# Two-layer trunk: quarters at the layers' turn in two-tile pieces, the state product in the inner product's bank, three yT sets

## The chip, the cores and the metric

The kernel runs on one core of one Trainium2 chip. The metric is the device time of one execution in microseconds (us), lower is better. A core has TensorE (matmuls; PE in rows), VectorE (DVE), ScalarE (ACT), GpSimd (POOL) and SyncE (SP), each with its own instruction stream in program order; SyncE here issues most DMAs. Matmul results land in PSUM banks, everything else lies in SBUF, and GpSimd cannot be given work on PSUM here: all its operands are SBUF tiles.

## The reference

1024 tokens of width 1024 pass two layers. Each computes `h = RMSNorm(x)*(1+scale)+shift`, `y = mixer(h)`, `x = x + gate*RMSNorm(y)`. Layer 0 mixes by differential attention, layer 1 by retention, which in chunks of 64 tokens is:

```python
inner = einsum("bnihd,bnjhd->bnhij", q, k) * intra_decay       # gamma^|i-j|
inner_out = einsum("bnhij,bnjhe->bnihe", inner, v)
def step(state, qkv):
    cross = einsum("bihd,bhde->bihe", q_c * query_decay, state)  # gamma^i
    state = chunk_decay * state + einsum("bjhd,bjhe->bhde", k_c * key_decay, v_c)
out = head_rms_norm(inner_out + cross)     # 4 heads, q/k 256 wide, v 512 wide
y = silu(g) * out ; result = y @ w_out
```

All is float32; the kernel keeps the accuracy by splitting each float32 operand in a high and a low float16 part and adding three products (high·high, high·low, low·high).

## The kernel before, in words

Tokens are handled in eight tiles of 128 rows. One program runs layer 0, the turn to layer 1, layer 1's four heads one after the other, and the last output projection. TensorE holds nearly all the time, and the other engines prepare for it.

**The turn.** After attention, `out0(t)` makes the output projection of tile t (48 matmuls of 512 columns on line 562), squares and sums it (ACT, line 574), takes the root on POOL (lines 576, 577, 140), adds the residual (DVE, 579), and normalizes the rows once more into `x1` (ACT 291, POOL 292 and 140, DVE 614). `out0_yT(t)` turns tile t's mixer output first: two casts and one transposing DMA on SP (line 602). `out0_hT(g)` then makes layer 1's input: `x1` of four token tiles is transposed on TensorE (line 310), scaled and shifted on ACT (629) and cast to two float16 parts, plain (`hA`, `hB`) and as sums and differences (`hS`, after subtracts on DVE, lines 630 to 634); the casts are lines 640 (ACT) and 641 (DVE). Layer 1's input projections use a two-by-two block scheme with seven products instead of eight, hence these sums, and hence sums of weight blocks too: four adds on POOL (line 759) for each set of columns, before the casts of the weights (ACT 772, DVE 773). `PRODUCTS` gives the order of the seven: the first two need `hA` and `hB` only, the third and fourth need `hS`.

The order of all this is a string: each letter is a function, each digit its argument, and each engine executes in that order, apart from what the scheduler interleaves:

```python
order = ("... b7 f0 y5 o3 o4 y6 o5 h0 y7 o6 o7 h1")   # y: out0_yT, o: out0, h: out0_hT
```

**Retention.** For each head come the seven products of the q/k columns (line 799, 256 columns each), those of v, and those of the gate. In the gate's seven steps, behind the second half of a step, stands a step of retention, `retention(n)`: `scores` of a span (line 946, times a decay table on DVE, line 952, then casts 953 and 954), `state` of the span before (line 968: keys times decayed values, added to a running state by DVE 974 or 976, cast 978 and 979), and `outputs` (inner product, line 989, in one bank; state product, line 999, in another). ACT brings the state product times the query decay to SBUF (1003), DVE adds the inner product (1004), and DVE normalizes (1007).

**The tail.** `gated` multiplies with silu(gate). The last projection (line 1120) needs `yT(t)`: two transposing DMAs from DRAM `y_d` (heads 0 to 2, line 1106) and two from head 3's own result (1108), in one of two buffers that bear the tags of `qT` and `kT`, so tile 0's may start when head 3 has read `qT` for the last time. Its weights arrive through SP (line 1092) in sixteen pieces, and are cast on ACT (1096) and DVE (1097), in the order in which the first token tile needs them: 36 matmuls for output half 0, 36 for half 1, then twelve each with head 3.

## Time and profile before

| | before |
|---|---|
| median of 3 runs | 1405.28 us (1404.12 to 1405.83) |
| the profiled execution | 1402.77 us, span 1400.8 us |
| TensorE busy | 1299.1 us, granted clock 0.981 |
| VectorE, ScalarE, GpSimd busy | 929.3, 670.0, 261.0 us |

The profiled execution is one run, 2.5 us below the median. The span is the traced part of it. A view of waits lists, for each engine, how long it stood idle and what it waited for last; a timeline lists an engine's instructions in order of time, consecutive ones of a line together, with the idle time ahead in brackets; a table of stretches gives each engine's busy time in it and TensorE's granted clock (1.0 is the upper of its two levels, 2.4 GHz; 1.2 GHz is 0.5).

### The profile page before, as it was taken

The numbers are of one execution on the slowest core, as the hardware profiler recorded it, in microseconds if no ns is written. First come the engines' busy times: TensorE is split into PE (matmuls) and PEld (weight loads), VectorE is DVE, ScalarE is ACT, GpSimd is POOL, SyncE is SP. The second block draws the span as 40 slices with busy tenths as digits, with TensorE's granted clock in tenths as the row PEclk, the third lists the DMA queues.
The fourth block names the chain that finished last, engine by engine and source line by source line (L and its number), as shares of the span: only waits on it lengthen the run. The fifth ranks groups of instructions, "written<-read, shape, count | busy, mean of one in ns | idle before, by whom it ended". The sixth has DMA issues, their size and how long they took to land. (4 is left out here: it accounts for less than half of the span.)

```text
span 1400.8 us, 21197 instructions
## 1 busy us (share of the span) xinstructions
PE 1299.1 (93%) x8273; PEld 776.8 (55%) x8273; DVE 929.3 (66%) x1734; ACT 670.0 (48%) x1250; POOL 261.0 (19%) x318
## 2 busy tenths in 40 slices
PE   4899999899999997896899999999999999799998
PEld 2445455445545444355786658665866586544443
DVE  4866996997986777666558765876587648831011
ACT  4855544654654655366354644454445445720000
POOL 2000110101101222520223122322232220100000
PEclk9999999999999999898999999999999999999999
DMA  9723554656452466631212242223222333474350
GB/s 298 244 69 70 131 120 115 143 126 134 102 128 52 126 148 132 151 109 49 69 60 76 84 128 62 76 83 117 73 76 74 103 92 121 119 154 97 97 121 30
DMA packets 244372, 152.60 MB, mean 109 GB/s; under 512 B 142840, under 2 KB 233136, under 8 KB 244272
## 3 DMA queue, kind: packets, MB, share of 16 engines
q1 hardware_dynamic: 241168, 140.24, 38.8%
q0 software_dynamic: 3104, 11.02, 2.6%
q8 instruction: 64, 1.05, 0.3%
q14 instruction: 36, 0.29, 0.1%
HBM read 101.95 MB, written 14.68 MB: 83 GB/s over the span
## 5 line engine op out<-in xcount | busy, mean ns | idle before, releaser
L773 DVE SCALAR_TENSOR_TENSOR w<-raw,w 128x1024 f16<-128x1024 f32 x82 | 121.8, 1489 | 88.7 <-ACT w L772 88.6
L331 PE MATMUL ps_mm<-w,hT 128*128 128x512 f16 x768 | 175.7, 379 | 0.0
L1120 PE MATMUL ps_mm<-wo,yT 128*128 128x512 f16 x768 | 167.8, 382 | 4.2 <-DMA yT<-y_d 4.2
L799 PEld LDWEIGHTS <-hS 128*128 128x128 f16 x1536 | 150.1, 98 | 20.9
L759 POOL TENSOR_TENSOR raw<-raw,raw 128x1024 f32<-128x1024 f32 x48 | 126.8, 2642 | 186.7 <-DVE w L773 183.5
L319 PE MATMUL ps_mm<-hT,w 128*128 128x512 f16 x624 | 142.2, 379 | 0.0
L799 PE MATMUL ps_mm<-w,hS 128*128 128x256 f16 x1152 | 130.3, 273 | 0.0
L1120 PEld LDWEIGHTS <-yT 128*128 128x128 f16 x768 | 75.3, 98 | 96.6 <-DMA yT<-y_d 5.2
L511 ACT ACTIVATE sb<-sb,mx 128x128 f32<-128x128 f32 (+7 forms) x128 | 98.2, 768 | 63.5 <-DVE mx L504 62.9
L331 PEld LDWEIGHTS <-hT 128*128 128x128 f16 x768 | 74.2, 98 | 82.5
L799 PEld LDWEIGHTS <-w 128*128 128x128 f16 x744 | 75.2, 101 | 78.3 <-issue 13.6
L772 ACT ACTIVATE w<-raw 128x1024 f16<-128x1024 f32 x82 | 85.8, 1049 | 39.8 <-issue 15.0
L575 DVE TENSOR_TENSOR po<-ps_mm,gp 128x512 f32<-128x512 f32 x16 | 11.1, 691 | 132.0 <-ACT junk L574 132.0
L562 PE MATMUL ps_mm<-w_o,yT 128*128 128x512 f16 x384 | 93.4, 394 | 4.8 <-DVE x L575 3.6
L319 PEld LDWEIGHTS <-w 128*128 128x128 f16 x624 | 60.1, 98 | 67.5
L504 DVE CUSTOM_DVE_ANT_0 sb<-ps_sc,table 128x512 f32<-128x512 f32 (+3 forms) x128 | 73.2, 584 | 33.5 <-PE ps_sc L501 26.1
L574 ACT ACTIVATE junk<-ps_mm 128x512 f16<-128x512 f32 x32 | 19.0, 595 | 154.5 <-PE ps_mm L1120 145.0
L799 PE MATMUL ps_mm<-w,hA 128*128 128x256 f16 x768 | 86.6, 273 | 0.0
L799 PEld LDWEIGHTS <-hA 128*128 128x128 f16 x768 | 75.1, 98 | 9.9
L292 POOL TENSOR_SCALAR ss<-ss 128x1 f32<-128x1 f32 x48 | 19.1, 398 | 300.2 <-ACT junk L291 288.5
L799 PE MATMUL ps_mm<-hS,w 128*128 128x512 f16 (+1 forms) x312 | 63.0, 362 | 12.0 <-ACT held L807 12.0
L169 DVE SCALAR_TENSOR_TENSOR acc<-raw,cond,acc 128x256 f32<-128x256 f32 x140 | 65.7, 480 | 7.8 <-DMA raw<-in_ada_w 6.2
(202 smaller groups left out, 2247.0 us busy)
## 6 DMA issues: line engine op xcount, KB each, us to landing
raw<-in_ret_w_in SPq DMA_DIRECT2D x60, 512.0 KB, 3.6
raw<-in_ada_w SPq DMA_DIRECT2D x40, 512.0 KB, 6.6
raw<-in_da_w_in SPq DMA_DIRECT2D x16, 1024.0 KB, 5.8
raw1o<-in_ret_w_out SPq DMA_DIRECT2D x16, 512.0 KB, 4.5
y_d<-y SPq DMA_DIRECT2D x6, 1024.0 KB, 4.7
x<-in_x SPq DMA_DIRECT2D x8, 512.0 KB, 7.5
raw<-in_ada_w SPq DMA_DIRECT2D x4, 1024.0 KB, 5.3
raw_o<-in_da_w_out SPq DMA_DIRECT2D x4, 1024.0 KB, 5.1
```

Source lines behind the costliest of these rows:

```text
L169: nc.vector.scalar_tensor_tensor(out=acc, in0=parts[k], scalar=cond[:, k : k + 1], in1=acc, op0=ALU.mult, op1=ALU.add)
L292: nc.gpsimd.tensor_scalar(out=ss[:, 3:4], in0=ss[:, 0:1], scalar1=scale / n, scalar2=eps, op0=ALU.mult, op1=ALU.add)
L319: nc.tensor.matmul(ps, w[:, k, wi, lo : lo + P], hT[k][g][:, xi, :], start=(k == 0 and wi == 0 and xi == 0), stop=(k == NK - 1 and wi == 1),)
L331: nc.tensor.matmul(ps, hT[k][g][:, xi, j * P : (j + 1) * P], w[:, k, wi, :], start=(k == 0 and wi == 0 and xi == 0), stop=(k == NK - 1 and ...
L504: nc.vector.tensor_tensor_reduce(out=sb[:, c, k], in0=ps[c][:, 0:n], in1=table[:, S - L + lo : S - L + lo + n], scale=-es, scalar=(3.0e38 ...
L511: nc.scalar.activation(out=sb[:, c, 0:L], in_=sb[:, c, 0:L], func=AF.Exp, scale=-1.0, bias=mx[:, m0 + c : m0 + c + 1], accum_out=z[:, 4 * ...
L562: nc.tensor.matmul(ps, yT(yi, k), wo[k // 4][:, k % 4, wi, n * 512 : (n + 1) * 512], start=(k == 0 and yi == 0 and wi == 0), stop=(k == NK ...
L759: add = lambda o, x: nc.gpsimd.tensor_tensor(out=r[o], in0=r[o], in1=r[x], op=ALU.add)
L772: nc.scalar.activation(out=w[:, :, 0, :], in_=r[name], func=AF.Copy, scale=SW)
L773: nc.vector.scalar_tensor_tensor(out=w[:, :, 1, :], in0=r[name], scalar=SW, in1=w[:, :, 0, :], op0=ALU.mult, op1=ALU.subtract)
L799: nc.tensor.matmul(ps[:, pc], l, r, start=(first and i == 0 and k == 0 and wi == 0 and xi == 0), stop=(k == 3 and wi == 1), skip_group_che ...
L1120: nc.tensor.matmul(ps[n], yT1[t][:, yi, k, :], wo1[k // 4, n][:, k % 4, wi, :], start=(k == 0 and yi == 0 and wi == 0), stop=(k == 15 and ...
```

## The change

Three parts are changed at once.

1. **The turn.** `out0_hT` is called four times, for two token tiles each, instead of twice for four. Its pieces take buffers of their own (`early` and `ys` tags that are done with) in place of attention's "v" buffers. The subtracts run on GpSimd for the first three calls and on VectorE for the last. `hS` is laid out in other tiles. The order string has the four calls spread: one behind tile 3's projection, one behind tile 4's, one behind tile 6's, one at the end.
2. **Retention.** The last span (two tiles) becomes two of one. The state product is the first to be written into the inner product's bank, and the inner product adds to it; the passes of lines 1003 and 1004 are gone. For that, the query decay is folded in a second decay table for the scores and in the norm's epsilon. Scores come earlier: those of the first span in v's products, the others between the two halves of a gate step; state and outputs follow the second half. There is a fourth `kN`, and one more state per head.
3. **The tail.** `yT` has three sets in turn (four `held` buffers, and the `qT` and `kT` tags) and takes six transposing DMAs per tile (8, 8, 4 and 4 blocks from `y_d`, 4 and 4 from head 3) in place of four.

The diff, cut to its core:

```diff
-SST = 2.0**4
+SA1 = 2.0
...
-SPANS = ((0, 2), (2, 1), (3, 1), (4, 1), (5, 1), (6, 2))
+SPANS = ((0, 2), (2, 1), (3, 1), (4, 1), (5, 1), (6, 1), (7, 1))
+DECS = RC + P + 3
...
-        out[h, :, RC : RC + 2] = np.exp(log_gamma * i) * (RQK**-0.5 * SA * SV / (SQK1 * SST))
...
+        out[h, :, RC : RC + P] = np.where(p // CHUNK <= u1 // CHUNK, c * SA1 * np.exp(log_gamma * (np.abs(u1 - p) - u1)), 0.0)
+        out[h, :, RC + P] = HEAD_EPS * np.exp(-2.0 * log_gamma * p[:, 0])
...
-    def out0_hT(g):
-        if g == 0:
+    def out0_hT(j):
+
+        if j == 0:
...
-        n = slice(g * 256, (g + 1) * 256)
-        for k in range(4):
-
-            t = att.tile([P, 8, 256], F32, name="hq", tag="v", bufs=2)
+        n = slice(j * P, (j + 1) * P)
+        for kh in range(2):
+
+            pa, ta, ba = (early, "qs", 2) if j == 0 else (ys, f"y{2 * j - 2 + kh}", 1)
+            pb, tb, bb = (early, "ks", 2) if j < 2 else (ys, f"y{2 * j - 4 + kh}", 1)
+            t = pa.tile([P, 4, 2, P], F32, name="hq", tag=ta, bufs=ba)
+            t2 = pb.tile([P, 4, 2, P], F32, name="hq2", tag=tb, bufs=bb)
             for i in range(2):
...
+                for kk in range(2):
+                    k = 2 * kh + kk + 4 * i
+                    for b in range(2):
+                        c = (2 * kk + b) * P
+                        nc.tensor.transpose(out=ps[:, c : c + P], in_=xns[2 * j + b][:, k * P : (k + 1) * P], identity=ident)
+                    m = mods[1, k]
+                    nc.scalar.activation(
...
+            eng = nc.vector if j == 3 else nc.gpsimd
+            for i in range(2):
+                eng.tensor_tensor(out=t2[:, i], in0=t[:, 1], in1=t[:, 3 * i], op=ALU.subtract)
+            eng.tensor_tensor(out=t2[:, 2], in0=t[:, 0], in1=t2[:, 1], op=ALU.subtract)
+            eng.tensor_tensor(out=t2[:, 3], in0=t[:, 2], in1=t2[:, 2], op=ALU.subtract)
...
-        "o1 b5 a6 a7 b6 y4 o2 b7 f0 y5 o3 o4 y6 o5 h0 y7 o6 o7 h1"
+        "o1 b5 a6 a7 b6 y4 o2 b7 f0 y5 o3 h0 o4 y6 h1 o5 y7 o6 h2 o7 h3"
...
-            for c in range(NC - 1):
-                kn = ret.tile([P, 2, 2, 2, P], F16, name="kN", tag="kN", bufs=3)
+            for c in range(NC):
+                kn = ret.tile([P, 2, 2, 2, P], F16, name="kN", tag="kN", bufs=4)
...
+                    if n == 5 and u == 1:
+                        scores(*SPANS[0])
...
                 o = av()
+                if t0 > 0:
+                    c, u = part(t)
+                    for m in range(2):
+                        for qi, si in ((0, 0), (0, 1), (1, 0)):
+                            nc.tensor.matmul(
+                                o, st["qT"][:, c, m, qi, u], sts[t0][:, m, si, :],
+                                start=(m == 0 and qi == 0 and si == 0), stop=False,
+                            )
...
-                    nc.scalar.activation(out=dst, in_=x, func=AF.Copy, scale=st["dec"][:, RC + i : RC + i + 1])
-                    nc.vector.tensor_tensor(out=dst, in0=o, in1=dst, op=ALU.add)
...
+                s0, eps = (SA1 * SV, st["dec"][:, RC + P : RC + P + 1]) if t0 > 0 else (SA * SV, HEAD_EPS)
+                r = row_rsqrt(o, RV, 1.0 / s0**2, eps)
+                nc.vector.tensor_scalar(out=y1[t // 4][:, t % 4, :], in0=o, scalar1=r, scalar2=1.0 / s0, op0=ALU.mult, op1=ALU.mult)
...
+                    if u == 0 and n + 1 < len(SPANS):
+                        scores(*SPANS[n + 1])
                     if u == 1:
-                        retention(n)
+                        if n + 1 < len(SPANS):
+                            state(*SPANS[n])
+                        outputs(*SPANS[n])
...
-        yT = ret.tile([P, 2, 16, P], F16, name="yT", tag=("qT", "kT")[t % 2], bufs=1)
+        if t % 3 == 0:
+            ps_ = [held(F16, [P, 8, P]) for _ in range(4)]
+        else:
+            yt = ret.tile([P, 4, 8, P], F16, name="yT", tag=("qT", "kT")[t % 3 - 1], bufs=1)
+            ps_ = [yt[:, i] for i in range(4)]
+        for i in range(2):
+            for b in range(2):
+                if i == 0:
+                    nc.sync.dma_start(out=ps_[b], in_=y_d[:, t, b, 0:2, :].rearrange("p h e -> p (h e)"), transpose=True)
+                else:
+                    nc.sync.dma_start(out=ps_[2 + b][:, 0:4, :], in_=y_d[:, t, b, 2, :], transpose=True)
...
-            nc.sync.dma_start(out=yT[:, b, 12:16, :], in_=last_y[t][:, b, :], transpose=True)
+            nc.sync.dma_start(out=ps_[2 + b][:, 4:8, :], in_=last_y[t][:, b, :], transpose=True)
```

Where the instructions stand. First POOL's stream at the turn. Before, the four adds of weight blocks (line 759) stand ahead of the root of tile 3's norm (lines 576, 577, 140), while the attention of the last heads ends:

```order
L759 TENSOR_TENSOR raw_6161<-raw_6161,raw_6165 128x1024
L759 TENSOR_TENSOR raw_6165<-raw_6165,raw_6167 128x1024
L759 TENSOR_TENSOR raw_6167<-raw_6167,raw_6161 128x1024
L759 TENSOR_TENSOR raw_6163<-raw_6163,raw_6167 128x1024
L597 DMA xres<-in_x 128x2x1024
L549 TENSOR_TENSOR sso<-sso,z 128x2
L576 TENSOR_TENSOR ss<-ss 128x1
L550 TENSOR_TENSOR sso<-sso,negh 128x2
L577 TENSOR_SCALAR ss<-ss 128x1
L140 TENSOR_TENSOR rs<-ss,negh 128x1
L612 DMA x_d<-xres 128x1024
L292 TENSOR_SCALAR ss<-ss 128x1
```

Now (line 779) they stand between the two parts of tile 5: its root (580, 581, 144) ahead, and the store of its residual (619) and the root of its `x1` (296, 144) behind:

```order
L580 TENSOR_TENSOR ss<-ss 128x1
L581 TENSOR_SCALAR ss<-ss 128x1
L144 TENSOR_TENSOR rs<-ss,negh 128x1
L779 TENSOR_TENSOR raw_6209<-raw_6209,raw_6213 128x1024
L779 TENSOR_TENSOR raw_6213<-raw_6213,raw_6215 128x1024
L779 TENSOR_TENSOR raw_6215<-raw_6215,raw_6209 128x1024
L779 TENSOR_TENSOR raw_6211<-raw_6211,raw_6215 128x1024
L619 DMA x_d<-xres 128x1024
L296 TENSOR_SCALAR ss<-ss 128x1
L144 TENSOR_TENSOR rs<-ss,negh 128x1
```

So tile 5's `x1` now comes behind four adds of 128x1024, which before were over ahead of tile 3's. Next, SP's queue at the tail, before: tile 1's transposes and then tile 0's (yT_12080), with the loads of the last weights (raw1o) between them:

```order
L1106 DMA_TRANSPOSE yT_12085<-y_d_102 128x12x128 x2
L1108 DMA_TRANSPOSE yT_12085<-y1_10860 128x4x128 x2
L1092 DMA raw1o_12054<-in_ret_w_out 128x2x512
L1106 DMA_TRANSPOSE yT_12080<-y_d_102 128x12x128
L1092 DMA raw1o_12058<-in_ret_w_out 128x2x512
L1106 DMA_TRANSPOSE yT_12080<-y_d_102 128x12x128
L1092 DMA raw1o_12063<-in_ret_w_out 128x2x512
L1108 DMA_TRANSPOSE yT_12080<-y1_10860 128x4x128
L1092 DMA raw1o_12067<-in_ret_w_out 128x2x512
L1092 DMA raw1o_12072<-in_ret_w_out 128x2x512
L1092 DMA raw1o_12076<-in_ret_w_out 128x2x512
```

And now, from the eleventh load of weights on; held_12122 and held_12123 are parts of tile 0's `yT`, yT_12130 is tile 1's, yT_12249 is tile 2's:

```order
L1106 DMA raw1o_12094<-in_ret_w_out 128x2x512
L1130 DMA_TRANSPOSE held_12122<-y1_10904 128x4x128
L1126 DMA_TRANSPOSE yT_12130<-y_d_102 128x8x128
L1130 DMA_TRANSPOSE held_12123<-y1_10904 128x4x128
L1126 DMA_TRANSPOSE yT_12130<-y_d_102 128x8x128
L1128 DMA_TRANSPOSE yT_12130<-y_d_102 128x4x128 x2
L1130 DMA_TRANSPOSE yT_12130<-y1_10904 128x4x128 x2
L1130 DMA_TRANSPOSE yT_12249<-y1_10904 128x4x128 x2
L1106 DMA raw1o_12098<-in_ret_w_out 128x2x512
L1106 DMA raw1o_12103<-in_ret_w_out 128x2x512
L1106 DMA raw1o_12107<-in_ret_w_out 128x2x512
```

Ten transposes, those of head 3's part of tiles 0 to 2 and all of tile 1, now stand ahead of the last five loads (three of the five are shown). Third, DVE in head 0 around the score table of span (4, 1). Before, a_7413 stands behind a cast of weights (773) and the normalizing of a row tile from SBUF (1007):

```order
L1004 TENSOR_TENSOR y_6646<-ps_av,y_6646 128x512
L169 SCALAR_TENSOR_TENSOR acc<-raw_7458,cond,acc 128x256
L773 SCALAR_TENSOR_TENSOR w_7475<-raw_7246,w_7475 128x4x256
L1007 TENSOR_SCALAR y_6646<-y_6646,rs 128x512
L952 TENSOR_TENSOR a_7413<-ps_sc,dec 128x128
L976 SCALAR_TENSOR_TENSOR st_7201<-st_7201,ps_sc 128x512
L773 SCALAR_TENSOR_TENSOR w_7574<-raw_7349,w_7574 128x4x256
L954 TENSOR_TENSOR aT<-a_7413,aT 128x128
L979 SCALAR_TENSOR_TENSOR sh<-st_7201,sh 128x512
L976 SCALAR_TENSOR_TENSOR st_7201<-st_7201,ps_sc 128x512
```

And now (a_7380) it stands behind two accumulating passes over adaLN weights (173), and 1027 reads the bank:

```order
L1027 TENSOR_SCALAR y_6696<-ps_av,rs 128x512
L1002 SCALAR_TENSOR_TENSOR sh<-st_7197,sh 128x512
L171 TENSOR_SCALAR acc<-raw_7545,cond 128x256
L173 SCALAR_TENSOR_TENSOR acc<-raw_7545,cond,acc 128x256
L974 TENSOR_TENSOR a_7380<-ps_sc,dec 128x128
L173 SCALAR_TENSOR_TENSOR acc<-raw_7545,cond,acc 128x256
L976 TENSOR_TENSOR aT<-a_7380,aT 128x128
L173 SCALAR_TENSOR_TENSOR acc<-raw_7545,cond,acc 128x256
L999 SCALAR_TENSOR_TENSOR st_7197<-st_7197,ps_sc 128x512 x2
L173 SCALAR_TENSOR_TENSOR acc<-raw_7547,cond,acc 128x256
```

In the new order 1004 is gone, and the state (999, before 976) comes behind the scores' second cast (976, before 954).

## Rows read from the trace of the kernel before

**Rows 1.** The page: the span, and busy time, share and instructions of TensorE.
```profile
span 1400.8 us, 21197 instructions
...
PE 1299.1 (93%) x8273; PEld 776.8 (55%) x8273; DVE 929.3 (66%) x1734; ACT 670.0 (48%) x1250; POOL 261.0 (19%) x318
```

**Rows 2.** TensorE's waits in the whole run: total us, times, longest us.
```profile
PE ps_sc L968 <- DVE a L952: 12.7, 9, 2.5
PE ps_mm L799 <- ACT held L807: 12.0, 4, 6.1
...
PE ps_av L989 <- ACT y L1003: 4.1, 3, 1.6
PE ps_mm L562 <- DVE x L575: 3.6, 1, 3.6
```

**Rows 3.** Stretches: us, busy us (xcount) of PE, PEld, DVE, ACT, POOL; granted clock.
```profile
760.00:770.00 10.00, 7.85 (x43) 4.77 (x43) 10.00 (x10) 2.78 (x6) 9.76 (x4) 0.83 0.05 15
1200.00:1210.00 10.00, 8.26 (x64) 5.85 (x63) 8.73 (x16) 7.65 (x14) 0.74 (x2) 1.00 0.63 172
582.00:627.00 45.00, 42.45 (x208) 20.55 (x207) 25.13 (x36) 23.26 (x43) 10.37 (x26) 0.97 0.48 128
```

**Rows 4.** Timeline of TensorE at the turn: start, length, line, count, [wait before].
```profile
579.58 8.04 PE L562 MATMUL ps_mm<-w_o,yT 128*128 128x512 f16 x24 [3.60 <-DVE x L575]
588.87 10.54 PE L562 MATMUL ps_mm<-w_o,yT 128*128 128x512 f16 x48 [1.25 <-DMA yT<-yh]
599.24 0.60 PE L310 MATMUL ps_sc<-ident,x 128*128 128x128 f32 x4
599.68 6.86 PE L562 MATMUL ps_mm<-w_o,yT 128*128 128x512 f16 x31
...
624.73 1.58 PE L799 MATMUL ps_mm<-hA,w 128*128 128x256 f16 x13
...
648.51 7.75 PE L799 MATMUL ps_mm<-hS,w 128*128 128x256 f16 x48 [6.05 <-ACT held L807]
```

**Rows 5.** Timeline of POOL at the turn.
```profile
563.31 12.26 POOL L759 TENSOR_TENSOR raw<-raw,raw 128x1024 f32<-128x1024 f32 x4 [2.26 <-DVE w L773]
```

**Rows 6.** Timeline of DVE at the turn.
```profile
573.41 5.52 DVE L773 SCALAR_TENSOR_TENSOR w<-raw,w 128x1024 f16<-128x1024 f32 x3
```

**Rows 7.** Timeline of DVE: tile 7's normalized rows.
```profile
630.43 0.75 DVE L614 TENSOR_SCALAR x<-xres,rs 128x1024 f32<-128x1024 f32 x1
```

**Rows 8.** Groups by line and shape: busy us, mean ns, idle before.
```profile
L629 ACT ACTIVATE hq<-ps_sc,mod 128x512 f32<-128x512 f32 x16 | 11.7, 771 | 3.1 <-DVE hS L641 1.5 <-DMA x_d<-xres 1.4
...
L640 ACT ACTIVATE hA<-hq 128x512 f16<-128x512 f32 x8 | 5.0, 628 | 0.2
```

**Rows 9.** Timeline of DVE beside POOL's adds, head 0.
```profile
759.33 2.56 DVE L1007 TENSOR_SCALAR y<-y,rs 128x512 f32<-128x512 f32 x1 [0.71 <-POOL rs L140]
...
762.02 0.67 DVE L976 SCALAR_TENSOR_TENSOR st<-st,ps_sc 128x512 f32<-128x512 f32 x1
...
771.70 0.49 DVE L1007 TENSOR_SCALAR y<-y,rs 128x512 f32<-128x512 f32 x1 [0.44 <-POOL rs L140]
```

**Rows 10.** Timeline of TensorE at the tail.
```profile
1220.60 1.46 PE L999 MATMUL ps_av<-sh,qT 128*128 128x512 f16 x6 [0.27 <-DVE y L1004]
1226.02 4.67 PE L1120 MATMUL ps_mm<-wo,yT 128*128 128x512 f16 x13 [3.97 <-DMA yT<-y_d]
1230.89 163.13 PE L1120 MATMUL ps_mm<-wo,yT 128*128 128x512 f16 x755 [0.20 <-DMA yT<-y_d]
```

**Rows 11.** SyncE's queue, line 1108: durations min/median/max ns, first and last start.
```profile
L1108 SPq DMA_TRANSPOSE yT<-y x16: 1188/1266/2514, 1211.0 to 1357.8; - x16
```

**Rows 12.** DMA of line 1092: time from issue to landing.
```profile
DMA to landing us min/median/max: 3.7/4.5/6.8
```

**Rows 13.** Groups by line and shape: the last weights' two casts.
```profile
L1097 DVE SCALAR_TENSOR_TENSOR wo<-raw1o,wo 128x1024 f16<-128x1024 f32 x16 | 19.4, 1220 | 4.8 <-ACT wo L1096 4.6
...
L1096 ACT ACTIVATE wo<-raw1o 128x1024 f16<-128x1024 f32 x16 | 16.6, 1052 | 11.1 <-DMA raw1o<-in_ret_w_out 9.7 <-PE ps_mm L799 1.4
```

More of the change, by code (lines that the diff above doesn't have):

```diff
@@ L728, in trunk @@
     ret = l1.enter_context(tc.tile_pool(name="ret", bufs=1, reuse_waits="tile"))
-    held = lambda: ret.tile([P, 2, 256], F32, name="held", tag="held", bufs=5)
+    held = lambda dtype=F32, shape=(P, 512): ret.tile(list(shape), dtype, name="held", tag="held", bufs=5)
     def raw_block(src):
@@ L977, in state @@
                 hi, lo = (sh[:, m, b, :] for b in range(2))
-                nc.scalar.activation(out=hi, in_=s32, func=AF.Copy, scale=SST / (SQK1 * SV))
-                nc.vector.scalar_tensor_tensor(out=lo, in0=s32, scalar=SST / (SQK1 * SV), in1=hi, op0=ALU.mult, op1=ALU.subtract)
+                nc.scalar.activation(out=hi, in_=s32, func=AF.Copy, scale=sst)
+                nc.vector.scalar_tensor_tensor(out=lo, in0=s32, scalar=sst, in1=hi, op0=ALU.mult, op1=ALU.subtract)
             sts[t0 + n] = sh
@@ L989, in outputs @@
                         nc.tensor.matmul(
-                            o, aT[t0 + j][:, ai, u], v[t0 + j][:, vi, :], start=(j == 0 and ai == 0 and vi == 0), stop=(j == i and ai == 1)
-                        )
-                dst = y1[t // 4][:, t % 4, :]
-                src = o
-                if t0 > 0:
-                    x = av()
-                    c, u = part(t)
-                    for m in range(2):
-                        for qi, si in ((0, 0), (0, 1), (1, 0)):
-                            nc.tensor.matmul(
-                                x, st["qT"][:, c, m, qi, u], sts[t0][:, m, si, :],
-                                start=(m == 0 and qi == 0 and si == 0), stop=(m == 1 and qi == 1),
-                            )
-                    nc.scalar.activation(out=dst, in_=x, func=AF.Copy, scale=st["dec"][:, RC + i : RC + i + 1])
-                    nc.vector.tensor_tensor(out=dst, in0=o, in1=dst, op=ALU.add)
-                    src = dst
-                r = row_rsqrt(src, RV, 1.0 / (SA * SV) ** 2, HEAD_EPS)
-                nc.vector.tensor_scalar(out=dst, in0=src, scalar1=r, scalar2=1.0 / (SA * SV), op0=ALU.mult, op1=ALU.mult)
-        def retention(i):
-            spans = (*SPANS, (NT, 0))
-            if i >= len(spans):
-                return
-            scores(*spans[i])
-            if 0 < i < len(SPANS):
-                state(*SPANS[i - 1])
-            if i > 0:
-                outputs(*SPANS[i - 1])
+                            o, aT[t0 + j][:, ai, u], v[t0 + j][:, vi, :],
+                            start=(t0 == 0 and j == 0 and ai == 0 and vi == 0), stop=(j == i and ai == 1),
+                        )
+                s0, eps = (SA1 * SV, st["dec"][:, RC + P : RC + P + 1]) if t0 > 0 else (SA * SV, HEAD_EPS)
+                r = row_rsqrt(o, RV, 1.0 / s0**2, eps)
+                nc.vector.tensor_scalar(out=y1[t // 4][:, t % 4, :], in0=o, scalar1=r, scalar2=1.0 / s0, op0=ALU.mult, op1=ALU.mult)
         def gated(u, ts):
@@ L1102, in out1_yT @@
     def out1_yT(t):
-        yT = ret.tile([P, 2, 16, P], F16, name="yT", tag=("qT", "kT")[t % 2], bufs=1)
+        if t % 3 == 0:
[9 more added lines that the diff above has]
+                    nc.sync.dma_start(out=ps_[2 + b][:, 0:4, :], in_=y_d[:, t, b, 2, :], transpose=True)
         for b in range(2):
-            nc.sync.dma_start(out=yT[:, b, 0:12, :], in_=y_d[:, t, b, 0:3, :].rearrange("p h e -> p (h e)"), transpose=True)
-        for b in range(2):
-            nc.sync.dma_start(out=yT[:, b, 12:16, :], in_=last_y[t][:, b, :], transpose=True)
-        yT1[t] = yT
+            nc.sync.dma_start(out=ps_[2 + b][:, 4:8, :], in_=last_y[t][:, b, :], transpose=True)
+        yT1[t] = ps_
     out1_yT(0)
```

52 lines of the change are left out of this document (27 added, 25 removed).

## The prediction

> **What bounds the kernel now.** I read the page first: TensorE is busy 1299.1 of the span's 1400.8 us, 93%, and no other engine is above 66% [rows 1]. So time comes or goes only where TensorE stands idle, runs at the lower clock, or gets more columns; 512 columns take 0.216 us (163.13 us for 755 matmuls, [rows 10]), and 128 columns a quarter of it, 0.054. The view of TensorE's waits comes next, to see which waits the change touches: 12.7 us in retention's state product, up to 2.5 us at a time, behind the score table's product on DVE; 4.1 us in the inner product, for ACT's pass of line 1003; 12.0 us in layer 1's products, behind ACT copies; and 3.6 us at the turn, behind DVE [rows 2]. Then the table of stretches, for what a wait costs besides itself: around the 2.5 us wait near 760 the granted clock of ten microseconds is 0.83 (0.17 of 10, so 1.7 us more), while around a wait of 1.75 us near 1207 it stays at 1.00 [rows 3]. I count 1.7 us for each wait of 2.5 us or more and none for shorter ones. Last, the timelines of the three places.
>
> **The turn, before.** Tile 4's projection waits 3.60 us for DVE, and tile 6's 1.25 us for a transposing DMA [rows 4]. The first is late because DVE's weight casts took 5.52 us for three while POOL added weight blocks [rows 5, 6]; such a cast alone takes 1.22 (the same operation and shape at the tail, [rows 13]). The last projection ends at 624.73, and the products with `hS` start only at 648.51, 23.8 us later [rows 4]. Of these, 6.45 us go for tile 7's own chain (its rows are normalized at 630.43 + 0.75 = 631.18, [rows 7]), and 17.3 us for four rounds of scaling, subtracting and casting for four tiles at once, ACT being the longest of them.
>
> **The turn, after.** Only the last two token tiles are left after tile 7's chain. ACT's part is eight scalings of 256 columns, each about half of 0.771, and six casts of 512 columns or so at 0.63 at most [rows 8]: 3.2 + 3.8 = 7.0, and with the first transposes, the wait for three subtracts in a row on DVE, and the copy that frees the bank I take 9.9. So `hS` is ready 6.45 + 9.9 = 16.4 us after tile 7's projection in place of 23.8: 7.4 us gained.
> When does tile 7's projection end? The DVE and DMA waits go (3.60 + 1.25), and 28 more transposes come before tile 5's end, 0.11 us each (four in 0.44 us, 599.24 to 599.68, [rows 4]), 3.1 us: tile 5 ends at 599.24 - 4.85 + 3.1 = 597.5. Its `x1` then needs a chain like tile 7's, 6.45 us, but with the four adds inside it. They took 12.26 us [rows 5]; about 2.5 of that lies beside the chain's own DVE and ACT steps, so `x1` of tile 5 is ready at 597.5 + 6.45 + 9.8 = 613.7, say 613. The third call needs it for its transposes, right behind tile 6's projection, which ends at 597.5 + 10.4 = 607.9 (48 matmuls of 0.216). So a **new wait of 5 us** stands there, with 1.7 us for the clock. Then 16 transposes (1.8 us), tile 7's 10.4 us: the end is at 613 + 1.7 + 1.8 + 10.4 = 627, 2.3 us later than 624.73. `hS` is ready at 627 + 16.4 = 643.4, 5.1 us ahead of 648.51.
> Bounds: with no such wait tile 7 ends near 620, and the turn gains 12. With POOL later by another 7 us the gain is gone and 2 us are lost.
> The 24 subtracts on POOL (128x256) do not show in this trace. The nearest row is the add of 128x1024, 12.26 / 4 = 3.07 us; scaled by elements it is 0.77 us, and unscaled 3.07. I take 0.77, since small and large operations of a POOL stream differ in the rows: the 26 operations between 582 and 627 took 10.37 us together [rows 3]. 24 x 0.77 + 12.3 + 10.4 = 41 us then fit into the 45 to 55 us that they have.
>
> **Retention.** Removed are 24 passes each on ACT (1003) and DVE (1004), and with them the wait of 4.1 us: nothing now stands between the inner product and the end of a bank. The 12.7 us are nine waits; the longest three come where POOL's adds slow DVE: there a normalizing pass from SBUF took 2.56 us, and 0.49 once POOL was done [rows 9]. In the new order the score table's product has half a gate step more (24 matmuls of 256 columns, 2.6 us) before anyone needs it, which is as long as the longest wait. I let 5.0 of the 12.7 stay: it still stands behind two passes of line 173, also with SBUF inputs, and the state's own DVE steps (976 before) can be late at the same place. So the waits shrink by 7.7 + 4.1 = 11.8, and 3 x 1.7 = 5.1 come back with the clock. Against that, per head six more matmuls of 512 columns for the extra state, three fewer in the inner product and six fewer score blocks of 128: 3 x 0.216 - 6 x 0.054 = 0.32, so 1.3 us in all. Sum: -11.8 - 5.1 + 1.3 = -15.6 us. Bounds: all of the 12.7 gone and the clock too gives -20.6; half of the waits kept and two of the three clock dips too gives about -10 + 2 = -8.
> A row in the same stretch weighs on how much stays: line 976, whose input lies in PSUM, took its usual 0.67 us at 762.02, between two slow ones [rows 9]. Line 1007 will read PSUM always, so it should take about 0.7 in place of 2.56 there. This speaks for the lower end; I leave it out of the sum, since line 173 comes into its place.
> The Trainium skill ("SBUF — State Buffer", section "SBUF: two separate sides") says that a DVE operation with two SBUF inputs and a GpSimd operation lock one port pair against each other for the whole instruction, whoever comes first. This trace agrees for the slow and the quick ones (2.56 beside 0.67). The rule speaks against subtracts on POOL; what they would do is priced under "half the gain".
>
> **The tail.** The wait for tile 0's transposes, 3.97 + 0.20 us, goes [rows 10], since they take buffers that are free long before, and the part of heads 0 to 2 is done during head 3. But the last five weight loads now stand behind ten transposes. Nine of these can start only when `qT` is last read, 0.65 us ahead of retention's end P (three inner matmuls follow now). At the median issue time of 1.27 us [rows 11] they take 11.4, so load 12 of 16 issues at P + 10.8, lands 4.5 us later [rows 12], and is cast in 1.05 + 1.22 [rows 13]: ready at P + 17.6. TensorE needs it after 54 matmuls, at P + 11.7. A **new wait of 5.9 us**; both old and new wait cost one clock dip, so the tail loses 5.9 - 4.2 = 1.7 us. Bounds: shortest issues (1.19) and landing (3.7) make the wait 4.4, so +0.2; longest landing (6.8) and two issues of 2.5 make it 10.7, so +6.5.
>
> **Sum.** -5.1 - 15.6 + 1.7 = -19.0 us on the profiled 1402.8 us gives 1383.8; the median lies 2.5 us above that execution, so 1386.3, and I forecast 1386.
>
> **The rivals.**
> *New waits smaller (0.22).* The adds get ahead of tile 5, or the loads are not late: for it speaks only that each margin is a few microseconds. Turn -12 without its wait, or tail -3 without its own: 1376 to 1381.
> *Half the gain (0.16).* Retention keeps -8, and the turn's wait is as long as what it saves: 1405.3 - 8 + 1.7 = 1399; with one of the two 1392. The mechanism is that DVE and POOL stand in each other's way, as in [rows 9]: at the turn DVE is busy 25.1 of 45 us [rows 3]; if each subtract holds up a DVE pass for its 0.77 us, 18.5 more make that 43.6 of 45, and what is late there is the casts for `hS`. Against it, the first three calls have some 15 us each before the next needs them.
> *No gain (0.05).* The state's DVE steps inherit the waits of the score product in full (12.7), the turn's and the tail's cancel: 1403 to 1406.
> *POOL bounds the turn (0.09), slower.* If a subtract costs as much as the whole add, 3.07 us, then POOL has 24 x 3.07 + 12.3 + 10.4 = 96 us of work in some 55: 41 us over. That adds 41 to a turn that gains nothing otherwise: 1405.3 - 15.6 + 1.7 + 41 = 1432. It decides from (55 - 22.7) / 24 = 1.35 us per subtract on, and the whole kernel is slower than before from 1.35 + 13.9 / 24 = 1.9 us on. The Trainium skill ("GPSIMD Engine Reference", section "Engine selection") advises against element-wise work with two inputs on GpSimd, about twice as slow as VectorE. A DVE pass of 1024 columns takes 1.22 us here [rows 13], so by that page a subtract of 256 would be an estimated 0.6 us, and POOL would not bound the turn.
>
> **Numbers.** The forecast has 0.48, from 1382 to 1391. The range must leave out no more than 2 in 10: from 1376 (without the lower half of the first rival) to 1399 (without the last two). The measurement of this kernel can tell 0.2%, 2.8 us, from no change. Faster by more: 0.48 + 0.22 + 0.16 = 0.86. Same 0.05. Slower 0.09.
>
> **What would show it.** In retention no wait above 1.5 us before the state product, and no lower clock at its POOL adds; the lines 1003 and 1004 absent. At the turn a wait of about 5 us behind tile 6's projection, for DVE's `x1`; POOL's subtracts near 0.77 us, its adds behind tile 5's root; `hS` products some 16 us after tile 7's projection. At the tail none for `yT(0)`, one of about 6 us within tile 0's second half, for a cast of `wo`. I would be wrong if the subtracts take over 1.4 us each, if state products still wait 2.5 us for DVE, or if the tail waits over 10 us.

## The result, and the profile after

The changed kernel took 1420.08 us (median of 4 runs, 1417.86 to 1421.59) against 1404.70 us before: ratio 1.0107, 95% interval 1.0090 to 1.0125. It is about 15 us slower, where 19 us less was forecast. The page of the changed kernel, its span and busy times, answers to [rows 1]:

```profile
span 1419.7 us, 21306 instructions
...
PE 1301.3 (92%) x8285; PEld 778.7 (55%) x8285; DVE 918.2 (65%) x1722; ACT 665.5 (47%) x1262; POOL 283.5 (20%) x342
```

TensorE has 2.2 us more of busy time, and the span is 18.9 us longer: the loss is mostly idle time. TensorE's waits (total us, times, longest), which answer to [rows 2]:

```profile
PE ps_sc L991 <- DVE a L974: 24.1, 12, 5.1
...
PE ps_sc L643 <- DVE x L621: 9.3, 3, 6.7
PE ps_sc L643 <- ACT hq L645: 9.0, 7, 2.3
PE ps_mm L819 <- ACT held L827: 8.9, 2, 5.4
...
PE ps_mm L1142 <- ACT wo L1110: 6.3, 1, 6.3
...
PE ps_mm L1142 <- DVE wo L1111: 4.0, 2, 3.3
```

Line 991 is 968 of before, 819 is 799, 643 is 310, 1142 is 1120. Before, TensorE's wait for ACT's scalings was:

```profile
PE ps_sc L310 <- ACT hq L629: 6.6, 8, 2.6
```

The waits of 4.1 us in the inner product and 4.2 us for `yT` are gone as forecast. In their place the waits ahead of the state product have doubled, from 12.7 to 24.1 us, with a longest of 5.1 in place of 2.5; the turn has 9.3 us in three waits for tile rows (`x1`) and 9.0 for ACT's scalings (6.6 before), the tail one of 6.3 and two of 4.0 together for casts of weights.

Three points in time divide the loss: the first `hS` products, the end of retention, and the end. In the profiled runs the first comes at 652.20 against 648.51 [rows 4], the second at 1234.3 against 1222.1 [rows 10], the third at 1419.7 against 1400.8. So the turn is 3.7 us longer, retention 8.6 (582.1 against 573.5), the tail 6.7 (185.4 against 178.7); forecast were -5.1, -15.6 and +1.7.

**Retention.** Head 0 of the changed kernel on three engines, in the order TensorE, VectorE, GpSimd (timeline: start, length, line, [idle before]):

```profile
777.60 0.81 PE L991 MATMUL ps_sc<-y,kN 128*128 128x512 f16 x3
782.94 1.03 PE L991 MATMUL ps_sc<-y,kN 128*128 128x512 f16 x3 [4.53 <-DVE a L974]
```

```profile
766.10 2.65 DVE L173 SCALAR_TENSOR_TENSOR acc<-raw,cond,acc 128x256 f32<-128x256 f32 x2
...
771.90 1.28 DVE L1002 SCALAR_TENSOR_TENSOR sh<-st,sh 128x512 f16<-128x512 f32 x2
781.14 0.75 DVE L1027 TENSOR_SCALAR y<-ps_av,rs 128x512 f32<-128x512 f32 x1 [7.96 <-POOL rs L144]
781.81 0.42 DVE L246 TENSOR_TENSOR gbias<-ps_tr,gbias 128x256 f32<-128x256 f32 x1
782.26 0.42 DVE L247 SCALAR_TENSOR_TENSOR gp<-gbias,gp 128x256 f32<-128x256 f32 x1
782.60 0.28 DVE L974 TENSOR_TENSOR a<-ps_sc,dec 128x128 f32<-128x128 f32 x1
```

```profile
765.60 2.35 POOL L779 TENSOR_TENSOR raw<-raw,raw 128x1024 f32<-128x1024 f32 x1 [1.20 <-DVE w L793]
772.50 7.72 POOL L779 TENSOR_TENSOR raw<-raw,raw 128x1024 f32<-128x1024 f32 x3 [4.56 <-DMA raw<-in_ret_w_in]
...
780.56 0.55 POOL L144 TENSOR_TENSOR rs<-ss,negh 128x1 f32<-128x1 f32 x1
```

Read it backwards. The second half of the state product waits 4.53 us for the PSUM bank that the score table's product (line 974) reads, and that product starts at 782.60. TensorE had its input ready long before. It stands on VectorE behind a normalizing pass (1027) that waited 7.96 us for the root on POOL (144), and POOL gave that root at 780.56 only, since it had three adds of weight blocks ahead of it, and ahead of them a wait of 4.56 us for a load. VectorE was idle for nearly 8 us, and for the last 6 of them the score product's input was ready behind the pass (its matmuls end at 775.1). The adds also stand later than before, when all four were over at 770.4: the load they wait for was issued at 768.78 (757.51 before), right behind VectorE's two slow passes of line 173 (766.10 to 768.75). The same shows in heads 1 (5.13 us) and 2 (4.53 us). The clock adds to it, in the two stretches of that place (columns as in [rows 3]):

```profile
774.00:784.00 10.00, 5.47 (x45) 4.01 (x43) 2.45 (x6) 1.68 (x4) 7.49 (x6) 0.97 0.00 0
784.00:794.00 10.00, 10.00 (x69) 6.76 (x68) 6.07 (x11) 3.70 (x7) 0.81 (x2) 0.86 0.24 69
```

**The turn.** TensorE, then POOL's adds, then ACT:

```profile
612.33 0.27 PE L643 MATMUL ps_sc<-ident,x 128*128 128x128 f32 x1
619.32 0.90 PE L643 MATMUL ps_sc<-ident,x 128*128 128x128 f32 x3 [6.72 <-DVE x L621]
...
630.28 0.44 PE L643 MATMUL ps_sc<-ident,x 128*128 128x128 f32 x2 [2.13 <-ACT hq L645]
...
635.95 2.78 PE L819 MATMUL ps_mm<-hA,w 128*128 128x256 f16 x24
...
652.20 7.78 PE L819 MATMUL ps_mm<-hS,w 128*128 128x256 f16 x48 [3.44 <-ACT held L827]
```

```profile
605.56 11.14 POOL L779 TENSOR_TENSOR raw<-raw,raw 128x1024 f32<-128x1024 f32 x4
```

```profile
628.69 0.63 ACT L660 ACTIVATE hS<-hq 128x512 f16<-128x512 f32 x1 [2.00 <-POOL hq L653]
629.23 1.00 ACT L645 ACTIVATE hq<-ps_sc,mod 128x256 f32<-128x256 f32 x2
```

The wait of 6.72 us behind tile 6's projection is there, for tile 5's rows, which POOL's four adds hold up (605.56). The last projection ends at 635.95, and the `hS` products follow 16.3 us later. But the transposes of each of the first three calls also wait some 2 us for ACT's scalings (1.77, 2.01 and 2.13 us): ACT stands at a cast whose input a POOL subtract has not finished (2.00 us at 628.69) and the next scalings are queued behind it. (In the last call, whose subtracts are on VectorE, TensorE waits 3.1 us for ACT too.) The subtracts by form (mean ns behind the busy time), and one of the last call's:

```profile
L651 POOL TENSOR_TENSOR hq<-hq 128x256 f32<-128x256 f32 x12 | 10.0, 836 | 16.2 <-ACT hq L645 16.2
...
L652 POOL TENSOR_TENSOR hq<-hq,hq 128x256 f32<-128x256 f32 x6 | 7.6, 1273 | 0.5
```

```profile
645.10 0.42 DVE L652 TENSOR_TENSOR hq<-hq,hq 128x256 f32<-128x256 f32 x1
```

**The tail.** TensorE and SyncE's queue:

```profile
1234.32 8.15 PE L1142 MATMUL ps_mm<-wo,held 128*128 128x512 f16 x37
1245.76 3.83 PE L1142 MATMUL ps_mm<-wo,held 128*128 128x512 f16 x17 [3.30 <-DVE wo L1111]
1255.93 0.59 PE L1142 MATMUL ps_mm<-wo,held 128*128 128x512 f16 x1 [6.34 <-ACT wo L1110]
```

```profile
1236.57 1.20 SPq L1130 DMA_TRANSPOSE held<-y  x1
1237.86 1.25 SPq L1126 DMA_TRANSPOSE yT<-y_d  x1
1239.51 1.20 SPq L1130 DMA_TRANSPOSE held<-y  x1
...
1244.73 5.20 SPq L1130 DMA_TRANSPOSE yT<-y  x4
1250.02 7.51 SPq L1106 DMA_DIRECT2D raw1o<-in_ret_w_out  x5
```

Retention ends at 1234.3, and the last projection starts at once. It stops at its 38th matmul for a cast on VectorE (3.30 us), which stands behind the gating there, and at its 55th for one on ACT (6.34), whose load was issued at 1250.02, behind the ten transposes. The first of the ten started at 1236.57; by the view of waits SyncE itself stood 3.7 us ahead of a transpose of line 1130 for ACT's gating, and 1.3 for VectorE's normalizing pass.

### The profile page after: what moved, and what is told of

It is laid out like the page before. It is cut to its first block, busy times and chain, and to the rows that moved or that the text cites. A ratio compares the mean times of both kernels' runs of the same rounds, so it can differ in the third digit from the quotient of the medians.

```text
span 1419.7 us, 21306 instructions
## 1 busy us (share of the span) xinstructions
PE 1301.3 (92%) x8285; PEld 778.7 (55%) x8285; DVE 918.2 (65%) x1722; ACT 665.5 (47%) x1262; POOL 283.5 (20%) x342
## 4 chain that ended last, share of the span: by engine, by line
PE 33%; DVE 9%; issue 3%; DMA 3%; ACT 3%; POOL 3%; SPq 1%; POOLq 0%; DVEq 0%; ACTq 0%
PE ps_mm L819 15%; PE ps_mm L1142 11%; PE ps_tr L819 4%; DVE w L793 2%; POOL raw L779 2%; DMA raw<-in_ada_w 2%; PE ps_av L1014 1%; DVE y L938 1%; DVE acc L173 1%; DVE sg L833 1%; DVE vr L929 1%; DMA raw<-in_ret_w_in 1%; ACT w L792 1%; PE ps_sc L991 1%; PE ps_av L1021 1%
## 5 line engine op out<-in xcount | busy, mean ns | idle before, releaser
L793 DVE SCALAR_TENSOR_TENSOR w<-raw,w 128x1024 f16<-128x1024 f32 x82 | 118.1, 1440 | 97.8 <-ACT w L792 97.8
L779 POOL TENSOR_TENSOR raw<-raw,raw 128x1024 f32<-128x1024 f32 x48 | 122.4, 2549 | 207.2 <-DVE w L793 189.9
L1142 PE MATMUL ps_mm<-wo,yT 128*128 128x512 f16 x480 | 104.1, 379 | 0.0
L1142 PEld LDWEIGHTS <-yT 128*128 128x128 f16 x480 | 47.0, 98 | 56.6
L173 DVE SCALAR_TENSOR_TENSOR acc<-raw,cond,acc 128x256 f32<-128x256 f32 x140 | 70.9, 517 | 7.1 <-DMA raw<-in_ada_w 5.6
L1142 PE MATMUL ps_mm<-wo,held 128*128 128x512 f16 x288 | 65.3, 388 | 10.3 <-ACT wo L1110 6.3
```

Of the source, the lines that this page charges most:

```text
L173: nc.vector.scalar_tensor_tensor(out=acc, in0=parts[k], scalar=cond[:, k : k + 1], in1=acc, op0=ALU.mult, op1=ALU.add)
L779: add = lambda o, x: nc.gpsimd.tensor_tensor(out=r[o], in0=r[o], in1=r[x], op=ALU.add)
L793: nc.vector.scalar_tensor_tensor(out=w[:, :, 1, :], in0=r[name], scalar=SW, in1=w[:, :, 0, :], op0=ALU.mult, op1=ALU.subtract)
L1142: nc.tensor.matmul(ps[n], yT1[t][2 * (k // 8) + yi][:, k % 8, :], wo1[k // 4, n][:, k % 4, wi, :], start=(k == 0 and yi == 0 and wi == 0), ...
```

## The experiments

Each kernel was timed beside the kernel before on the same chip; "before" is its median there. These medians run from 1403.0 to 1405.1 us, so a difference of 2 us between kernels of different chips is not clear.

**One part of the change taken back at a time.** The old turn (`h_part`, `out0_hT` and the order string of before):

```diff
-        "o1 b5 a6 a7 b6 y4 o2 b7 f0 y5 o3 h0 o4 y6 h1 o5 y7 o6 h2 o7 h3"
+        "o1 b5 a6 a7 b6 y4 o2 b7 f0 y5 o3 o4 y6 o5 h0 y7 o6 o7 h1"
```

> The changed kernel with the turn of before (two calls of four token tiles, subtracts on VectorE, old order string); retention and tail as changed. In the trace of the changed kernel the first hS products begin 3.7 us later than before (652.2 against 648.5). Theory (the three parts lose independently): 3.5 us less than the changed kernel, about 1416.5. Rival (the parts interact: the new turn's later weight preparation is what makes retention late): 8 us less or more, below 1412. If the turn of the change costs nothing by itself: 1420.

1416.99 us (before 1404.61; ratio 1.0094, 1.0076 to 1.0112): 3 us less than the change, as the theory has it, though the two intervals overlap; in the profiled run the first `hS` products come at 649.25 in place of 652.20.

The old retention (spans, decay table, scores ahead of the state, two banks):

```diff
-                    if u == 0 and n + 1 < len(SPANS):
-                        scores(*SPANS[n + 1])
                     if u == 1:
-                        if n + 1 < len(SPANS):
-                            state(*SPANS[n])
-                        outputs(*SPANS[n])
+                        retention(n)
```

> The changed kernel with retention of before (six spans, two banks, ACT and DVE passes between them, scores ahead of the state in the same half step); turn and tail as changed. Theory: from the first hS products to the last retention matmul the changed kernel takes 8.6 us more than before, so this is 8.5 less than the changed kernel, about 1411.5, with state product waits of 12.7 us and inner product waits of 4.1 us back. Rival (retention's accumulation gains as predicted and the loss there is caused by the other two parts): slower than the changed kernel, 1425 or more.

1407.12 us (before 1404.61; 1.0019, 1.0010 to 1.0029): 13 us less than the change. Retention's part costs more than the theory's 8.5, since the old one also leaves the tail less to wait for (5.1 us for ACT's cast in place of 6.3, 0.9 for VectorE's in place of 4.0). That the loss comes from the other two parts alone is out.

The old tail:

```diff
+        yT = ret.tile([P, 2, 16, P], F16, name="yT", tag=("qT", "kT")[t % 2], bufs=1)
```

> The changed kernel with the tail of before (two buffers with the tags of qT and kT, four transposes per tile). Theory (the tail's loss is the last five weight loads behind ten transposes, and casts behind the gating): 6 us less than the changed kernel, about 1414, with the wait for yT of some 4 us back, and the 6.3 us wait for a cast of wo gone or below 2. Rival (the tail is late since retention ends with DVE work still to do, in either buffering): the wait for casts stays at 3 to 10 us, and the time at 1420 or more.

1413.43 us (before 1404.61; 1.0066, 1.0053 to 1.0079): 6.7 us less than the change. Of the tail's waits only one is left:

```profile
PE ps_mm L1134 <- DMA yT<-y_d: 4.9, 1, 4.9
```

One at a time the three parts give back 3.1, 13.0 and 6.7 us, 22.7 together, more than the loss of 15.4: they do not add up, so the theory that they lose independently does not hold.

**GpSimd's adds.** 44 of the 48 adds of weight blocks on VectorE (all but the first set's):

```diff
+            eng = nc.gpsimd if self.place else nc.vector
-            add = lambda o, x: nc.gpsimd.tensor_tensor(out=r[o], in0=r[o], in1=r[x], op=ALU.add)
+            add = lambda o, x: eng.tensor_tensor(out=r[o], in0=r[o], in1=r[x], op=ALU.add)
```

> The changed kernel with the 44 adds of weight blocks of all sets but the first on VectorE in place of GpSimd. Theory (the three waits of 4.5 to 5.1 us ahead of the state product come from the score table's product standing on DVE behind a normalizing pass, whose root stands on POOL behind these adds): those three waits and their clock dips go, about 14 + 5 us, and DVE's 44 x 1.2 us more cost a few back: 1402 to 1407. Rival (the score product is late because of DVE's own work ahead of it, weight casts and sums of v and gate): waits before the state product grow from 24 us to 30 or more, time 1420 to 1430.

1384.01 us (before 1404.61; 0.9855, 0.9833 to 0.9876): 36 us less than the change, twice what the theory gave. The waits (total, times, longest):

```profile
PE ps_mm L820 <- ACT held L828: 3.4, 1, 3.4
...
PE ps_sc L992 <- DVE a L975: 1.9, 4, 1.3
```

The state product's waits fall from 24.1 to 1.9 us, and 5.4 of the 8.9 behind held go as well; TensorE's busy time falls by 11.7 us for the same matmuls.

Only the twelve adds that fall into the gate phase:

```diff
+            self.next_q = 0 < lo < D
...
-            add = lambda o, x: nc.gpsimd.tensor_tensor(out=r[o], in0=r[o], in1=r[x], op=ALU.add)
+            eng = nc.vector if self.next_q else nc.gpsimd
+            add = lambda o, x: eng.tensor_tensor(out=r[o], in0=r[o], in1=r[x], op=ALU.add)
```

> The changed kernel with only the twelve adds of the q/k weight sets of heads 1 to 3 on VectorE; these are the adds that fall into the gate phase, beside retention's steps. Theory (POOL's queue: root behind adds, normalizing pass behind root, score product behind that pass): the waits of 4.5 to 5.1 us and their clock dips go, and with them the smaller ones that stand behind slowed passes of line 173: about 20 us less than the changed kernel, 1398 to 1402. Rival (every add slows DVE beside it, wherever it stands, and the sum counts): a quarter of what all 44 adds gave (36 us), so 9 us, about 1411.

1397.95 us (before 1405.11; 0.9955, 0.9941 to 0.9968): 22 us less than the change, a little more than the theory's. The rest of the 36 us is in the other 32 adds.

```profile
PE ps_sc L993 <- DVE a L976: 7.0, 7, 1.5
```

The kernel before, with the same 44 adds on VectorE:

> The kernel before with the same 44 adds on VectorE, nothing else changed. Theory (nearly all of the 12.7 us of waits before the state product, three clock dips and 5.4 us behind held came from these adds, and accumulating in one bank is worth only the 4.1 us wait less 1.3 us of columns): 1380 to 1386, no slower than the changed kernel with them (1384), which bears a turn and a tail that are 3.7 and 6.7 us longer. Rival (accumulating gains by itself what was forecast, some 12 to 15 us, once the adds are out of its way): 1392 or more.

1395.41 us (before 1405.11; 0.9934, 0.9915 to 0.9953). The theory failed here: the old order keeps its waits with the adds off POOL, in six places in place of nine and up to 4.0 us long.

```profile
PE ps_sc L969 <- DVE a L953: 12.6, 6, 4.0
...
PE ps_av L990 <- ACT y L1004: 4.2, 3, 1.6
```

But their cause is another: in heads 0 to 2 the score product (line 953) now stands on VectorE behind two of the moved adds, which ends in waits of 4.01, 2.61 and 2.68 us. In head 0:

```profile
753.27 1.22 DVE L760 TENSOR_TENSOR raw<-raw,raw 128x1024 f32<-128x1024 f32 x1
756.00 1.23 DVE L760 TENSOR_TENSOR raw<-raw,raw 128x1024 f32<-128x1024 f32 x1 [1.51 <-DMA raw<-in_ret_w_in]
757.14 0.28 DVE L953 TENSOR_TENSOR a<-ps_sc,dec 128x128 f32<-128x128 f32 x1
```

With the same adds the changed kernel is 11 us faster, though it bears the longer turn and tail: scores that come half a step earlier leave room for such adds. What accumulating is worth with no add ahead of the scores this run does not show.

**A queue or shared ports.** All adds stay on GpSimd; only the normalizing pass moves to ACT, with the norm's constant folded in:

```diff
-                nc.vector.tensor_scalar(out=y1[t // 4][:, t % 4, :], in0=o, scalar1=r, scalar2=1.0 / s0, op0=ALU.mult, op1=ALU.mult)
+                nc.scalar.activation(out=y1[t // 4][:, t % 4, :], in_=o, func=AF.Copy, scale=r)
```

> The changed kernel with all adds on GpSimd as in the change, but retention's normalizing pass on ACT in place of VectorE. Theory (a queue: the score product stands on DVE behind a pass that waits for POOL): the waits before the state product fall from 24 us to 12 or less though every add is where it was, and the time to 1402 to 1410; some of it may return as ACT's waits. Rival (POOL's adds slow DVE beside them, through shared ports, and that makes the score product late): the waits stay at 18 us or more and the time above 1413.

1392.81 us (before 1404.27; 0.9913, 0.9898 to 0.9928): 27 us less than the change, by one instruction per token tile and head on another engine. The waits and the busy times:

```profile
PE ps_sc L991 <- DVE a L974: 3.3, 4, 0.9
```

```profile
PE 1292.6 (93%) x8285; PEld 775.6 (56%) x8285; DVE 902.6 (65%) x1690; ACT 682.4 (49%) x1294; POOL 291.5 (21%) x342
```

With every add on the engine where it was, the waits fall from 24.1 to 3.3 us: it was the queue. The wait for the root is still there, on ACT (here in head 0), and TensorE no longer stands behind it:

```profile
778.65 0.69 ACT L1027 ACTIVATE y<-ps_av,rs 128x512 f32<-128x512 f32 x1 [8.68 <-POOL rs L144]
```

The gain is larger than the theory's 10 to 18 us. (The pass also takes its 24.0 us of work off VectorE, whose busy time falls by 15.6; in the last kernel below, without adds on POOL, the same relief is worth nothing.) The busy time of TensorE is 8.7 us shorter for the same matmuls, at a granted clock of 0.984 in place of 0.979.

The same, with turn and tail of before, so that retention's part stands alone:

> Retention's part of the change alone, with the normalizing pass on ACT: the turn and the tail are those of before, all adds on GpSimd. Theory (what was forecast of retention, -15.6 us, holds once the score product no longer stands behind a pass that waits for POOL): 15 to 20 us less than before, 1384 to 1390. Rival (what the pass on ACT saved in the changed kernel, 27 us, only made up for what that kernel had lost, and accumulating is worth 3 us by itself): 1398 or more.

1387.30 us (before 1403.00; 0.9895, 0.9879 to 0.9910): 15.7 us less than before. In the profiled run retention itself takes 18.5 us less (555.1 against 573.5), and the tail gives 2.0 of it back, with a wait for `yT` of 6.5 us in place of 4.2.

```profile
PE ps_sc L975 <- DVE a L958: 3.3, 4, 1.0
```

**The turn.** All 48 adds on VectorE, the first set's too:

> The changed kernel with all 48 adds on VectorE, the first set's four too, which at the turn stand between tile 5's root and its rows. Theory (the turn's wait of 6.7 us is these four adds): against the same kernel with 44 adds on VectorE (1384.0) the wait for x1 of tile 5 goes, with its clock dip, so 7 to 9 us less, about 1376. Rival (tile 5's rows are late for DVE's sake, which now has the adds too): the wait stays at 4 us or more, 1382 or more.

1378.72 us (before 1405.11; 0.9822, 0.9803 to 0.9841): 5 us less than with 44, where the theory had 7 to 9. TensorE's wait for tile 5's rows is gone (9.3 us for `x1` become 2.6), ACT's scalings cost 10.5 in place of 9.0.

With the tail of before as well:

> The changed kernel with all 48 adds on VectorE and the tail of before. Theory (the new tail loses by itself, whatever retention does ahead of it): 6 us less than the 1378.7 of the same kernel with the new tail, about 1373, with one wait of 4 to 5 us for yT in place of 9 us for casts of wo. Rival (with retention's end now less crowded the new tail costs nothing): 1378 to 1380.

1374.43 us (before 1404.27; 0.9782, 0.9767 to 0.9798), 4 us less: the new tail loses whatever stands ahead of it.

And then the turn's subtracts on VectorE:

```diff
-            eng = nc.vector if j == 3 else nc.gpsimd
+            eng = nc.vector
```

> As the kernel with all adds on VectorE and the old tail, and the 24 subtracts of the turn's first three calls on VectorE too. Theory (at the turn TensorE waits 10 us for ACT's scalings, since ACT stands at casts that wait for POOL's subtracts, 0.7 to 1.6 us each): 4 to 7 us less than without this, about 1367. Rival (ACT is late for its own work, or DVE now is): within 2 us of it, or slower.

1367.64 us (before 1404.27; 0.9735, 0.9720 to 0.9749), 6.8 us less, with half of ACT's wait left:

```profile
PE ps_sc L643 <- ACT hq L645: 5.3, 6, 2.1
...
PE ps_sc L643 <- DVE x L621: 4.0, 2, 2.1
```

The old turn in place of the new, with adds on VectorE and the old tail:

> As the kernel with all adds on VectorE and the old tail, but with the turn of before. Theory (with the adds off POOL the new turn gains what was forecast): 3 to 6 us slower than with the new turn, about 1377; the wait for DVE of 3.6 us goes in the old turn too, so not more. Rival (the new turn gains nothing): 1373 or less.

1374.07 us (before 1404.27; 0.9782, 0.9768 to 0.9797), no different from the new turn with its subtracts on POOL; the theory, 3 to 6 us slower, failed. The new turn gains only with the subtracts on VectorE, and then 6 us, of which about 2 lie in the tail (a wait for `yT` of 7.1 us in place of 5.0).

**The tail.** The last five loads on GpSimd's queue (44 adds on VectorE):

```diff
-                nc.sync.dma_start(
+                (nc.gpsimd if 2 * i + j > 10 else nc.sync).dma_start(
```

> The changed kernel with 44 adds on VectorE and the last five weight loads of the tail issued on GpSimd's queue in place of SyncE's, where they stand behind ten transposes. Theory (loads behind transposes): against the same kernel without it (1384.0) the wait of 6 to 7 us for a cast of wo goes, the one of 3.3 us for DVE stays: about 1377. Rival (the loads wait for their buffers, which the casts of earlier weights free late, whatever queue they are on): a wait of 4 us or more stays, 1381 or more.

1384.31 us (before 1405.11; 0.9851, 0.9830 to 0.9873), no gain. The wait for ACT's cast falls from 7.2 to 2.7 us, but VectorE's rise, and other waits come behind it:

```profile
PE ps_mm L1143 <- DVE wo L1112: 5.2, 4, 3.3
...
PE ps_mm L1143 <- ACT wo L1111: 2.7, 1, 2.7
```

On that queue four of the five loads waited for a buffer that a cast on VectorE frees, 4.6 us in all, and the five took 10.3 us to land (median), where the changed kernel's sixteen on SyncE took 4.7. So the transposes are out of the way, but buffers and landing come next, and this run does not tell what the place in the queue alone costs. The next kernel leaves out the last five loads; their casts read the eleventh load's buffer in their place (all 48 adds on VectorE):

> The changed kernel with all adds on VectorE (1378.7 us), new tail, without the last five loads of output weights: their casts read the buffer of the eleventh load instead, so those five weight blocks are wrong values. Theory (of the tail's 9 us of waits, 5 to 6 come from these loads, by their place in the queue, their buffers and their landing, and 3.3 from casts behind the gating on DVE): waits for casts of 3 to 5 us in all stay, 1372 to 1375. Rival (all of it is DVE and ACT work that comes at once behind retention's end): waits of 8 us or more stay, 1378.

1369.07 us (before 1403.00; 0.9755, 0.9741 to 0.9769), against 1378.72 with them; measured beside before on each chip, 0.7% less, and 3 us below the theory's range.

```profile
PE ps_mm L1144 <- DVE wo L1113: 3.2, 2, 2.9
```

Only the casts behind the gating are left, 3.2 us of 9.3: the loads as a whole are the larger share of the tail's wait, by their place in the queue, their buffers and their landing together. TensorE's busy time fell by 2.1 us too.

**What the findings point to.** All adds and subtracts on VectorE, the old tail, the pass on ACT:

> All adds and subtracts on VectorE, the tail of before, the changed turn and retention, and the normalizing pass on ACT. Theory (with no adds on POOL the pass waits for nothing long, so moving it to ACT changes little; it takes 24 us off VectorE): within 3 us of the same with the pass on VectorE (1367.6), 1365 to 1369. Rival (VectorE is the second bound here now that it has the adds): 1362 or less.

1367.29 us (before 1403.00; 0.9740, 0.9726 to 0.9754). It beats both kernels by 2.6% and more, and is the same as with the pass on VectorE: once POOL has no adds, the pass has nothing to wait for, and VectorE's relief alone is worth nothing there.

## Why the prediction was wrong, point by point

- **Retention, -15.6 forecast, +8.6 measured: the step that failed** is "I let 5.0 of the 12.7 stay". Its two reasons named what stands on VectorE ahead of the score product by its length (two passes of line 173) and left out the normalizing pass by what it waits for. In place of 5.0, 24.1 us of waits were measured, and the prediction's own sign of being wrong, a state product that waits 2.5 us for DVE, came true with 5.1. The pass appears in the rows ahead of the prediction, at 771.70, behind POOL's adds [rows 9], and there it cost nothing, since the next score product's matmuls came only after it. Moving the scores half a step earlier put them in its wait, and the condition "no one on VectorE waits for POOL ahead of the scores" was not looked at. That POOL's adds start late here, behind a wait of 4.56 us for a load, may have a part in it too; no run isolates that. The other half of the step holds: without that queue, with the pass on ACT, 3.3 us of waits stay and the part alone measured -15.7 us. That this is so near to -15.6 is in part luck: retention gained 18.5 us there and the tail lost 2.0. The lower bound of -8 does not come out of its terms, either: half of 12.7, 4.1 and one clock dip of 1.7 less 1.3 of columns make -10.9.
- **The clock.** The forecast took 1.7 us for each of three waits, 5.1 in all. With the pass on ACT 20.8 us of waits went, three of them over 2.5 us, and 8.7 us of busy time came back: the right order, but too low.
- **The turn, -5.1 forecast, +3.7 measured.** The new wait for tile 5's rows was forecast as 5 us and measured 6.72; the 16.4 us from tile 7's projection to the `hS` products measured 16.3. What failed is the end of that projection, 627 forecast and 635.9 measured, and mostly by the subtracts on POOL: tile 6's projection already ended at 612.5 in place of 607.9, and in the two kernels with adds on VectorE and the old tail, subtracts on VectorE bring tile 7's end from 630.7 to 623.2. They took 0.84 to 1.27 us on average, not 0.77, and the sum asked whether POOL has time for them, not who waits for each. ACT waits in order for their results, and TensorE for ACT. The rival "POOL bounds the turn" had the right sign and the wrong mechanism: POOL has time, but its results come late. The Trainium skill ("GPSIMD Engine Reference", section "Engine selection") has such an operation about twice as slow on GpSimd as on VectorE; the trace has two to three times, 0.84 to 1.27 us against the 0.42 us of the last call's subtracts on VectorE.
- **The tail, +1.7 forecast, +6.7 measured.** The place was right, a cast of the twelfth load (5.9 us forecast, 6.34 and 0.67 measured). Two terms were missed. The load was issued 15.7 us after retention's end, not 10.8: the first of the ten transposes waits for ACT's gating and not for `qT` alone, so it started 2.3 us after the end and not 0.65 ahead of it, and all ten came behind that, where the sum has nine. And the cast behind the gating costs 3.3 us, which the forecast did not count at all.
- **Rivals.** None of them names what happened in retention. The parts do not cancel: each costs time beside the other two, and by much the same means, a queue that waits for another engine with ready work behind it.

## What to carry to other kernels

When work is moved earlier, look at what stands ahead of it on its engine, and ask of each such instruction not how long it takes but what it waits for: an instruction that waited at no cost before can hold up all that now follows it. A short operation on GpSimd that others wait for should not share that queue with long ones; of the two, either may move, and here moving the waiting pass to ACT or the long adds to VectorE each gave back more than the whole loss. (No run tries the pass on VectorE behind the score product.) Work that fits into an engine's free time can still be late for each of its readers, so cost it by its readers.
